# ReLU row sums: an opening block without its barrier, and another split of the last rows between ScalarE and VectorE

## The chip, the cores and the metric

The kernel runs on one core of a Trainium2 chip. The metric is the device time of one execution in microseconds (us). All executions quoted here are of the fast state, at a granted clock of 1.0. The kernel before had a median of 161.21 us (161.05 to 161.3, 3 runs). A profile is of one execution; its span runs from the first instruction to the last and is, in the kernel before, 1.3 to 1.4 us shorter than the execution's time.

## The reference

```python
x = np.random.randn(32, 512, 1024).astype(np.float32)
def reference(x):
    relu_x = np.maximum(x, 0)
    return np.sum(relu_x, axis=-1).astype(np.float32)
```

It reads 67.11 MB and writes 0.07 MB: 16384 rows of 1024 columns, one sum for each row. The data lie in 128 partitions (the lanes on which an engine works in parallel), so every partition has 128 rows.

## The kernel before

All loads are issued by SyncE, into three buffers of 16 rows per partition and, at the end, into two small tiles for pieces of a row. A load raises a semaphore, a counter for which the engines wait, once it has landed. In the body ScalarE clamps 7 to 16 rows at a time and VectorE reduces them. For the last rows each engine does whole rows by itself, with the sum as an accumulator output of the same instruction; the profile shows a second record for it, the accumulator read, which writes the sum out. The last four rows of a partition are treated apart: one for ScalarE, one for VectorE, the "split row", and the last row, which is ScalarE's. Of the split row 360 columns come with the two whole rows, the other 260 and 404 after the last row, as two loads of their own.

```python
TAIL = [8, 4]
PIECES = [360, 260, 404]
EARLY = 1
# ... (cut) ...
    first = PIECES[0]
    loaded = load(
        buf[:, :, :].rearrange("p c d -> p (c d)")[:, c * D : (c + 2) * D + first],
        rows(m, 3).rearrange("p c d -> p (c d)")[:, : 2 * D + first],
    )
    act_row(buf[:, c, :], m, loaded)
    dve_row(buf[:, c + 1, :], res[:, m + 1 : m + 2], loaded)
    last_loaded = load(buf[:, c + 3, :], rows(m + 3, 1)[:, 0, :])
    arrived = []
    col = first
    for part, w in zip(parts, PIECES[1:]):
        arrived.append(load(part[:, :w], rows(m + 2, 1)[:, 0, col : col + w]))
        col += w
    sums_done = n_act, n_dve
    act_row(buf[:, c + 3, :], m + 3, last_loaded)
    # ... the stores of the other rows' sums ...
    last, w = parts[-1], PIECES[-1]
    dve_row(buf[:, c + 2, :first], last[:, w : w + 1], None)
    for i in range(1, extra):
        dve_row(parts[i - 1][:, :], last[:, w + i : w + i + 1], arrived[i - 1])
    nc.vector.wait_ge(sems.dve, n_dve)
    nc.vector.tensor_scalar(out=last[:, :], in0=last[:, :], scalar1=0.0, scalar2=None,
        op0=MAX, op1=ADD, accum_out=res[:, NT - 2 : NT - 1],
    ).wait_op(arrived[-1], 16, "sem-ge").then_inc(sems.dve, 1)
    store(NT - 2, 2, n_act, n_dve)
```

The sums of the earlier pieces are written into extra columns behind the last piece (they are never negative, so the clamp leaves them alone), and the last instruction adds all up. It must wait for VectorE's own earlier writes, hence the `wait_ge` on VectorE's own semaphore.

The opening block of the program holds a barrier: each engine drains and waits for all the others. `EARLY = 1` puts the first load ahead of it:

```python
def issue_ahead_of_the_barrier(tc, n_loads):
    # ... (cut) ...
    loads = [i for i in body if i.engine == SP][:n_loads]
    for i in loads:
        body.remove(i)
    at = next(n for n, i in enumerate(opening) if i.engine == SP)
    opening[at:at] = loads
```

Of the kernel before, what the change touches and what calls it, by code (L numbers as in the profile page):

```python
# [4 lines left out]
F32 = mybir.dt.float32  # L5
# [12 lines left out]


TAIL = [8, 4]  # L20
PIECES = [360, 260, 404]

EARLY = 1

# [1 line left out]
def kernel(tc: tile.TileContext, x: bass.AP, out: bass.AP):  # L26
    nc = tc.nc
    sems = Semaphores(tc)

    tc.close()  # L30
    tc.compile()
    nc.cur_bb = nc.bb_map[tc.start_bb_name]
    body = nc.cur_bb.bb.instructions
    ends = list(body)
    body.clear()
    n_stores = relu_sum(nc, sems, x, out)
    body.extend(ends)


    nc.cur_bb = nc.bb_map[tc.start_bb_name + "_end"]  # L40
    nc.cur_bb.bb.instructions.clear()
    nums = sorted(s.num for s in (*sems.loads, sems.act, sems.dve))
    cleared = range(nums[0], nums[-1] + 1)
    assert len(cleared) == len(nums)
    nc.sync.sem_clear(cleared)
    nc.sync.wait_ge(sems.stored, 16 * n_stores).then_inc(sems.stored, -16 * n_stores)
    issue_ahead_of_the_barrier(tc, EARLY)


class Semaphores:  # L50
    def __init__(self, tc: tile.TileContext):
        n = len(TWO) + len(TAIL) + 1 + len(PIECES)
        self.loads = [tc.alloc_semaphore(f"load{i}") for i in range(n)]
        self.act = tc.alloc_semaphore("act")
        self.dve = tc.alloc_semaphore("dve")
        self.stored = tc.alloc_semaphore("stored")


def relu_sum(nc, sems: Semaphores, x: bass.AP, out: bass.AP):
    x_flat = x.flatten_outer_dims()  # L60
    N, D = x_flat.shape
    NT = N // P
    NB = len(TWO)
    assert N == P * NT == P * ROWS * (NB + 1)
    assert sum(TAIL) == ROWS - 4 and sum(PIECES) == D

    bufs = [nc.alloc_sbuf_tensor(f"io{i}", [P, ROWS, D], F32) for i in range(NBUF)]
    res = nc.alloc_sbuf_tensor("res", [P, NT], F32)
    extra = len(PIECES) - 1
    parts = [  # L70
        nc.alloc_sbuf_tensor(f"piece{i + 1}", [P, w + extra * (i + 1 == extra)], F32)
        for i, w in enumerate(PIECES[1:])
    ]


    N1 = P * ROWS
    xf = x_flat[:N1].rearrange("(p m) d -> p m d", p=P)
    xv = x_flat[N1:].rearrange("(p m) d -> p m d", p=P)
    o_flat = out.rearrange("b s -> (b s)")
    of = o_flat[:N1].rearrange("(p m) -> p m", p=P)  # L80
    ov = o_flat[N1:].rearrange("(p m) -> p m", p=P)

    def rows(m, n):
        if m < ROWS:
            return xf[:, m : m + n, :]
        return xv[:, m - ROWS : m - ROWS + n, :]

    def sums(m, n):
        if m < ROWS:
            return of[:, m : m + n], res[:, m : m + n]  # L90
        return ov[:, m - ROWS : m - ROWS + n], res[:, m : m + n]

    n_load = n_act = n_dve = n_store = 0

    def load(dst, src, after=None):
        nonlocal n_load
        dma = nc.sync.dma_start(out=dst, in_=src)  # L97
        if after:
            dma.wait_op(sems.dve, after[1], "sem-ge")
        dma.then_inc(sems.loads[n_load], 16)  # L100
        n_load += 1
        return sems.loads[n_load - 1]

    def store(m, n, act, dve):
        nonlocal n_store
        dst, src = sums(m, n)
        nc.sync.wait_ge(sems.act, act)
        nc.sync.dma_start(out=dst, in_=src).wait_op(sems.dve, dve, "sem-ge").then_inc(
            sems.stored, 16
        )  # L110
        n_store += 1

    def clamp(ap, loaded):
        nonlocal n_act
        i = nc.scalar.activation(out=ap, in_=ap, func=RELU)  # L115
        if loaded is not None:
            i.wait_op(loaded, 16, "sem-ge")
        i.then_inc(sems.act, 1)
        n_act += 1

    def total(ap, m, n):
        nonlocal n_dve
        nc.vector.tensor_reduce(  # L123
            out=res[:, m : m + n], in_=ap, axis=mybir.AxisListType.X, op=ADD
        ).wait_op(sems.act, n_act, "sem-ge").then_inc(sems.dve, 1)
        n_dve += 1

    def act_row(ap, m, loaded):
        nonlocal n_act
        i = nc.scalar.activation(  # L130
            out=ap, in_=ap, func=RELU, accum_out=res[:, m : m + 1]
        )
        if loaded is not None:
            i.wait_op(loaded, 16, "sem-ge")
        i.then_inc(sems.act, 1)
        n_act += 1

    def dve_row(ap, accum_out, loaded):
        nonlocal n_dve
        i = nc.vector.tensor_scalar(  # L140
            out=ap,
            in0=ap,
            scalar1=0.0,
            scalar2=None,
            op0=MAX,
            op1=ADD,
            accum_out=accum_out,
        )
        if loaded is not None:
            i.wait_op(loaded, 16, "sem-ge")  # L150
        i.then_inc(sems.dve, 1)
        n_dve += 1

    freed = []
    m = 0
    for j in range(NB):
        buf = bufs[j % NBUF]
        loaded = load(buf[:, :, :], rows(m, ROWS), j >= NBUF and freed[j - NBUF])
        c = 0
        act_waits = dve_waits = loaded  # L160
        for n in TWO[j]:
            clamp(buf[:, c : c + n, :], act_waits)
            total(buf[:, c : c + n, :], m + c, n)
            act_waits = None
            c += n
        for _ in range(ACT[j]):
            act_row(buf[:, c, :], m + c, act_waits)
            act_waits = None
            c += 1
        for _ in range(DVE[j]):  # L170
            dve_row(buf[:, c, :], res[:, m + c : m + c + 1], dve_waits)
            dve_waits = None
            c += 1
        assert c == ROWS
        freed.append((n_act, n_dve))
        m += ROWS


    buf = bufs[NB % NBUF]
    c = 0  # L180
    for n in TAIL:
        loaded = load(
            buf[:, c : c + n, :], rows(m, n), None if c else freed[NB - NBUF]
        )
        for i in range(n):
            if i % 2 == 0 or (n == 8 and i == 7):
                act_row(buf[:, c, :], m, loaded if i == 0 else None)
            else:
                dve_row(buf[:, c, :], res[:, m : m + 1], loaded if i == 1 else None)
            c += 1  # L190
            m += 1

    first = PIECES[0]
    loaded = load(
        buf[:, :, :].rearrange("p c d -> p (c d)")[:, c * D : (c + 2) * D + first],
        rows(m, 3).rearrange("p c d -> p (c d)")[:, : 2 * D + first],
    )
    act_row(buf[:, c, :], m, loaded)
    dve_row(buf[:, c + 1, :], res[:, m + 1 : m + 2], loaded)
    last_loaded = load(buf[:, c + 3, :], rows(m + 3, 1)[:, 0, :])  # L200
    arrived = []
    col = first
    for part, w in zip(parts, PIECES[1:]):
        arrived.append(load(part[:, :w], rows(m + 2, 1)[:, 0, col : col + w]))
        col += w
    sums_done = n_act, n_dve
    act_row(buf[:, c + 3, :], m + 3, last_loaded)



    store(0, ROWS, *freed[0])
    store(ROWS, NT - ROWS - 2, *sums_done)

    last, w = parts[-1], PIECES[-1]
    dve_row(buf[:, c + 2, :first], last[:, w : w + 1], None)
    for i in range(1, extra):
        dve_row(parts[i - 1][:, :], last[:, w + i : w + i + 1], arrived[i - 1])
    nc.vector.wait_ge(sems.dve, n_dve)  # L218
    nc.vector.tensor_scalar(  # L219
        out=last[:, :],  # L220
        in0=last[:, :],
        scalar1=0.0,
        scalar2=None,
        op0=MAX,
        op1=ADD,
        accum_out=res[:, NT - 2 : NT - 1],
    ).wait_op(arrived[-1], 16, "sem-ge").then_inc(sems.dve, 1)
    n_dve += 1
    store(NT - 2, 2, n_act, n_dve)
    return n_store  # L230


def issue_ahead_of_the_barrier(tc: tile.TileContext, n_loads: int):


    SP = mybir.EngineType.SP
    blocks = tc.nc.main_func.blocks
    opening = blocks[0].instructions
    body = next(b for b in blocks if b.name == tc.start_bb_name).instructions
    loads = [i for i in body if i.engine == SP][:n_loads]  # L240
    for i in loads:
        assert isinstance(i, mybir.InstDMACopy)
# [3 lines that stand above are left out]
# [30 lines left out]
```

## Time and profile before

| | before |
|---|---|
| span of the profiled execution | 159.6 us |
| DMA queue's packet time, share of the span | 98.1% |
| VectorE busy / ScalarE busy | 117.5 / 104.2 us |
| first compute (ScalarE starts on the first load) | 21.73 us |
| both engines start on the load with the two whole rows | 155.36 us |
| last sum ends | 158.17 us |

Below, "the row's start" is ScalarE's start on the first of the last four rows (155.36 here), and "the tail" is the time from there to the end of the last sum on either engine: 158.17 - 155.36 = 2.81 us. The profile lines are shown in the prediction.

### The profile page before, as it was taken

How to read it: one execution, taken by the hardware profiler on the slowest of the kernel's cores; microseconds unless marked ns; L12 is line 12 of the kernel's file. 1: busy time of each engine (PE TensorE's matmuls, PEld its weight loads, DVE VectorE, ACT ScalarE, POOL GpSimd, SP SyncE). 2: the span in 40 equal slices, each digit the busy share in tenths (PEclk: the TensorE clock that was granted, in tenths of full speed). 3: DMA queues.
4: the chain of work that ended last, by engine and by line, in shares of the span. 5: the costliest groups of instructions: out<-in, count | busy, mean ns of one | idle time of the engine just before them, and what ended most of it. 6: DMA issues, size and time to landing. Idle time of an engine off the chain costs nothing.

```text
span 159.6 us, 129 instructions
## 1 busy us (share of the span) xinstructions
DVE 117.5 (74%) x41; ACT 104.2 (65%) x50; POOL 0.2 (0%) x4
## 2 busy tenths in 40 slices
DVE  0000000009999499994999999999999999999986
ACT  3000059990799708996099941999339992499985
POOL 0000000000000000000000000000000000000000
DMA  7996996996996998979969969969969969798994
GB/s 263 525 525 263 525 526 263 525 525 263 526 493 296 525 411 378 525 328 460 526 279 509 525 263 526 525 263 525 525 263 525 509 279 525 337 452 386 412 405 127
DMA packets 2304, 67.18 MB, mean 421 GB/s; under 512 B 640, under 2 KB 896, under 8 KB 1024
## 3 DMA queue, kind: packets, MB, share of 16 engines
q1 hardware_dynamic: 2304, 67.18, 98.1%
HBM read 67.11 MB, written 0.07 MB: 421 GB/s over the span
## 4 chain that ended last, share of the span: by engine, by line
DMA 43%; DVE 34%; ACT 17%; another core or an unknown queue 3%; SPq 0%; issue 0%; DVEq 0%
DMA io<-in_x_dram 43%; DVE res L123 32%; ACT io L115 17%; DVE io L140 1%; SPq L97 0%; DVE piece L219 0%; DVE piece L140 0%; DVEq L218 0%
## 5 line engine op out<-in xcount | busy, mean ns | idle before, releaser
L123 DVE TENSOR_REDUCE res<-io 128x8 f32<-128x8192 f32 (+2 forms) x9 | 101.1, 11286 | 39.9 <-ACT io L115 39.9
L115 ACT ACTIVATE io<-io 128x8192 f32<-128x8192 f32 (+2 forms) x9 | 81.7, 9111 | 46.9 <-DMA io<-in_x_dram 46.9
L130 ACT ACTIVATE io<-io 128x1024 f32<-128x1024 f32 x20 | 20.9, 1045 | 5.9 <-DMA io<-in_x_dram 5.7
L140 DVE TENSOR_SCALAR_CACHE_REDUCE io<-io 128x1024 f32<-128x1024 f32 (+1 forms) x14 | 15.5, 1165 | 0.7 <-DMA io<-in_x_dram 0.6
L130 ACT ACTIVATION_READ_ACCUMULATOR io<-io 128x1 f32 x20 | 3.8, 188 | 0.0
L115 ACT ACT_TABLE_LOAD x1 | 1.3, 1283 | 0.8 <-PEq L260 0.8
L140 DVE DVE_READ_ACCUMULATOR io<-io 128x1 f32 x14 | 1.2, 82 | 0.0
L219 DVE TENSOR_SCALAR_CACHE_REDUCE piece<-piece 128x406 f32<-128x406 f32 x1 | 0.6, 576 | 0.1
L140 DVE TENSOR_SCALAR_CACHE_REDUCE piece<-piece 128x260 f32<-128x260 f32 x1 | 0.4, 424 | 0.0
L260 POOL MEMSET const-bfloat16-1.0<- 128x1 bf16 x1 | 0.1, 102 | 0.0
L260 POOL MEMSET const-uint8-127<- 128x1 uint8 x1 | 0.1, 102 | 0.0
L260 POOL MEMSET const-float32-0.0<- 128x1 f32 x1 | 0.1, 99 | 0.2 <-issue 0.2
L260 POOL MEMSET const-float32-1.0<- 128x1 f32 x1 | 0.1, 99 | 0.0
L140 DVE DVE_READ_ACCUMULATOR piece<-piece 128x1 f32 x1 | 0.1, 83 | 0.0
L219 DVE DVE_READ_ACCUMULATOR piece<-piece 128x1 f32 x1 | 0.1, 82 | 0.0
## 6 DMA issues: line engine op xcount, KB each, us to landing
io<-in_x_dram SPq DMA_DIRECT2D x1, 4096.0 KB, 21.6
io<-in_x_dram SPq DMA_DIRECT2D x1, 2048.0 KB, 26.1
io<-in_x_dram SPq DMA_DIRECT2D x1, 1204.0 KB, 28.6
io<-in_x_dram SPq DMA_DIRECT2D x1, 512.0 KB, 29.4
piece<-in_x_dram SPq DMA_DIRECT2D x1, 202.0 KB, 29.3
piece<-in_x_dram SPq DMA_DIRECT2D x1, 130.0 KB, 29.3
io<-in_x_dram SPq DMA_DIRECT2D x7, 26.9
out_dram<-res SPq DMA_DIRECT2D x1, 55.0 KB, 1.6
```

Source lines behind the costliest of these rows:

```text
L115: i = nc.scalar.activation(out=ap, in_=ap, func=RELU)
L123: nc.vector.tensor_reduce(out=res[:, m : m + n], in_=ap, axis=mybir.AxisListType.X, op=ADD).wait_op(sems.act, n_act, "sem-ge").then_inc(se ...
L130: i = nc.scalar.activation(out=ap, in_=ap, func=RELU, accum_out=res[:, m : m + 1])
L140: i = nc.vector.tensor_scalar(out=ap, in0=ap, scalar1=0.0, scalar2=None, op0=MAX, op1=ADD, accum_out=accum_out,)
L219: nc.vector.tensor_scalar(out=last[:, :], in0=last[:, :], scalar1=0.0, scalar2=None, op0=MAX, op1=ADD, accum_out=res[:, NT - 2 : NT - 1],) ...
L260: nc = _bacc.Bacc("TRN2", target_bir_lowering=False, num_devices=1)
```

## The change

Its intent is twofold: no barrier at the start, so that nothing waits for it; and a shorter way from the last landing to the last sum. ScalarE takes 180 columns of the split row, the row's last 190 columns come in one load with the last row (they are adjacent in memory; the load has 607 KB), and the middle comes last as pieces of 220 and 224 columns, so that the last instruction has 228 columns instead of 406.

```diff
-PIECES = [360, 260, 404]
+ACT_PIECE, DVE_PIECE, END_PIECE = 180, 210, 190
+PIECES = [220, 224]
 ...
+    loaded = load(flat[:, at : at + b], src[:, :b])
+    act_row(buf[:, c, :], res[:, m : m + 1], loaded)
+    sums_act = n_act
+    act_row(flat[:, at + split : at + a], others[0], None)
+    piece_act = n_act
+    dve_row(buf[:, c + 1, :], res[:, m + 1 : m + 2], loaded)
+    sums_dve = n_dve
+    dve_row(flat[:, at + a : at + b], others[1], None)
+    loaded = load(flat[:, at + end : at + 4 * D], src[:, end:])
+    act_row(buf[:, c + 3, :], res[:, m + 3 : m + 4], loaded)
+    nc.vector.wait_ge(sems.act, piece_act)
+    dve_row(flat[:, at + end : at + 3 * D], others[2], loaded)
+    arrived = []
+    for part, n in zip(parts, PIECES):
+        arrived.append(load(part[:, :n], src[:, b : b + n]))
+        b += n
 ...   (two stores, cut)
+    for i in range(len(PIECES) - 1):
+        dve_row(parts[i][:, :], others[3 + i], arrived[i])
 ...   (the last instruction and the last store stay as they were; most removed lines are cut)
+    for i in list(opening):
+        if isinstance(i, (mybir.InstDrain, mybir.InstEventSemaphore)):
+            opening.remove(i)
```

More of the change, by code (lines that the diff above doesn't have):

```diff
@@ L46 @@
     nc.sync.wait_ge(sems.stored, 16 * n_stores).then_inc(sems.stored, -16 * n_stores)
-    issue_ahead_of_the_barrier(tc, EARLY)
+    open_without_barrier(tc, EARLY)
 class Semaphores:
     def __init__(self, tc: tile.TileContext):
-        n = len(TWO) + len(TAIL) + 1 + len(PIECES)
+        n = len(TWO) + len(TAIL) + 2 + len(PIECES)
         self.loads = [tc.alloc_semaphore(f"load{i}") for i in range(n)]
@@ L64, in relu_sum @@
     assert N == P * NT == P * ROWS * (NB + 1)
-    assert sum(TAIL) == ROWS - 4 and sum(PIECES) == D
+    assert sum(TAIL) == ROWS - 4 and ACT_PIECE + DVE_PIECE + END_PIECE + sum(PIECES) == D
     bufs = [nc.alloc_sbuf_tensor(f"io{i}", [P, ROWS, D], F32) for i in range(NBUF)]
     res = nc.alloc_sbuf_tensor("res", [P, NT], F32)
-    extra = len(PIECES) - 1
+    extra = len(PIECES) + 2
     parts = [
-        nc.alloc_sbuf_tensor(f"piece{i + 1}", [P, w + extra * (i + 1 == extra)], F32)
-        for i, w in enumerate(PIECES[1:])
+        nc.alloc_sbuf_tensor(f"piece{i}", [P, w + extra * (i + 1 == len(PIECES))], F32)
+        for i, w in enumerate(PIECES)
     ]
@@ L126, in total, with act_row @@
         n_dve += 1
-    def act_row(ap, m, loaded):
+    def act_row(ap, accum_out, loaded):
         nonlocal n_act
-        i = nc.scalar.activation(
-            out=ap, in_=ap, func=RELU, accum_out=res[:, m : m + 1]
-        )
+        i = nc.scalar.activation(out=ap, in_=ap, func=RELU, accum_out=accum_out)
         if loaded is not None:
@@ L166, in relu_sum @@
         for _ in range(ACT[j]):
-            act_row(buf[:, c, :], m + c, act_waits)
+            act_row(buf[:, c, :], res[:, m + c : m + c + 1], act_waits)
             act_waits = None
@@ L186, in relu_sum @@
             if i % 2 == 0 or (n == 8 and i == 7):
-                act_row(buf[:, c, :], m, loaded if i == 0 else None)
+                act_row(buf[:, c, :], res[:, m : m + 1], loaded if i == 0 else None)
             else:
@@ L191, in relu_sum @@
             m += 1
-    first = PIECES[0]
-    loaded = load(
-        buf[:, :, :].rearrange("p c d -> p (c d)")[:, c * D : (c + 2) * D + first],
-        rows(m, 3).rearrange("p c d -> p (c d)")[:, : 2 * D + first],
-    )
-    act_row(buf[:, c, :], m, loaded)
-    dve_row(buf[:, c + 1, :], res[:, m + 1 : m + 2], loaded)
-    last_loaded = load(buf[:, c + 3, :], rows(m + 3, 1)[:, 0, :])
-    arrived = []
-    col = first
-    for part, w in zip(parts, PIECES[1:]):
-        arrived.append(load(part[:, :w], rows(m + 2, 1)[:, 0, col : col + w]))
-        col += w
-    sums_done = n_act, n_dve
-    act_row(buf[:, c + 3, :], m + 3, last_loaded)
-    store(0, ROWS, *freed[0])
-    store(ROWS, NT - ROWS - 2, *sums_done)
-    last, w = parts[-1], PIECES[-1]
-    dve_row(buf[:, c + 2, :first], last[:, w : w + 1], None)
-    for i in range(1, extra):
-        dve_row(parts[i - 1][:, :], last[:, w + i : w + i + 1], arrived[i - 1])
+    flat = buf[:, :, :].rearrange("p c d -> p (c d)")
+    src = rows(m, 4).rearrange("p c d -> p (c d)")
+    at = c * D
+    split = 2 * D
+    a, b = split + ACT_PIECE, split + ACT_PIECE + DVE_PIECE
+    end = split + D - END_PIECE
+    last, w = parts[-1], PIECES[-1]
+    others = [last[:, w + i : w + i + 1] for i in range(extra)]
+    loaded = load(flat[:, at : at + b], src[:, :b])
[3 more added lines that the diff above has]
+    piece_act = n_act
+    dve_row(buf[:, c + 1, :], res[:, m + 1 : m + 2], loaded)
+    sums_dve = n_dve
[4 more added lines that the diff above has]
+    dve_row(flat[:, at + end : at + 3 * D], others[2], loaded)
+    arrived = []
+    for part, n in zip(parts, PIECES):
+        arrived.append(load(part[:, :n], src[:, b : b + n]))
+        b += n
+    assert b == end
+    store(0, ROWS, *freed[0])
+    store(ROWS, NT - ROWS - 2, sums_act, sums_dve)
+    for i in range(len(PIECES) - 1):
+        dve_row(parts[i][:, :], others[3 + i], arrived[i])
     nc.vector.wait_ge(sems.dve, n_dve)
@@ L230, in relu_sum, with open_without_barrier @@
     return n_store
-def issue_ahead_of_the_barrier(tc: tile.TileContext, n_loads: int):
+def open_without_barrier(tc: tile.TileContext, n_loads: int):
     SP = mybir.EngineType.SP
```

## The prediction

> **What bounds the kernel now.** I read the page first, then the chain of work that ended last in order of time, then the timeline of the last 8 us and of the first two, and last the DMA issues.
>
> The page's load figures come first:
>
> ```profile
> DMA  7996996996996998979969969969969969798994
> ...
> q1 hardware_dynamic: 2304, 67.18, 98.1%
> HBM read 67.11 MB, written 0.07 MB: 421 GB/s over the span
> ```
>
> The DMA engines are busy 98.1% of the 159.6 us span. VectorE (74%) and ScalarE (65%) are not the bound of the body. Everything that the body computes lies beside the loads.
>
> The chain, in order of time (start us, us, what), shows where the bound starts and where it stops:
>
> ```profile
> 0.72 0.07 issue
> 0.79 40.24 DMA io<-in_x_dram
> 41.04 0.02 issue
> ...
> 126.77 28.57 DMA io<-in_x_dram
> 155.34 0.02 issue
> 155.36 1.68 DVE io L140 x4
> 157.03 0.43 DVE piece L140 x2
> 157.47 0.03 issue
> 157.49 0.02 DVEq L218
> 157.51 0.07 issue
> 157.58 0.58 DVE piece L219 x2
> ```
>
> Two things are to be seen. At the start, the load on the chain is the second one, issued at 0.79 after the barrier; it lands at 41.03, while the first one, issued at 0.00, has landed by 21.73, where ScalarE starts on it. The loads therefore stand in a queue: an 8.39 MB load lands every 41.04 - 21.73 = 19.3 us. At the end, from 155.34 on, a stretch of 159.6 - 155.3 = 4.3 us follows the large loads: a whole row on VectorE, three pieces of the split row, and the closing store. Only this stretch can be changed by another split.
>
> The timeline of that stretch (start us, us, engine line op tile) is what my sums rest on:
>
> ```profile
> 155.36 1.06 ACT L130 ACTIVATE io<-io 128x1024 f32<-128x1024 f32 x1 [0.45 <-DMA io<-in_x_dram]
> 155.36 1.22 DVE L140 TENSOR_SCALAR_CACHE_REDUCE io<-io 128x1024 f32<-128x1024 f32 x1 [0.57 <-DMA io<-in_x_dram]
> ...
> 156.50 0.52 DVE L140 TENSOR_SCALAR_CACHE_REDUCE io<-io 128x360 f32<-128x360 f32 x1
> ...
> 156.65 1.06 ACT L130 ACTIVATE io<-io 128x1024 f32<-128x1024 f32 x1
> ...
> 157.02 0.42 DVE L140 TENSOR_SCALAR_CACHE_REDUCE piece<-piece 128x260 f32<-128x260 f32 x1
> 157.37 0.08 DVE L140 DVE_READ_ACCUMULATOR piece<-piece 128x1 f32 x1
> 157.58 0.58 DVE L219 TENSOR_SCALAR_CACHE_REDUCE piece<-piece 128x406 f32<-128x406 f32 x1
> 157.62 0.19 ACT L130 ACTIVATION_READ_ACCUMULATOR io<-io 128x1 f32 x1
> 158.09 0.08 DVE L219 DVE_READ_ACCUMULATOR piece<-piece 128x1 f32 x1
> ```
>
> VectorE ends at 158.17, ScalarE at 157.81, so ScalarE has 0.36 us to spare. The store goes at 158.19 and takes 1.4 us to land.
>
> The landings come from the DMA issues (KB each, us from issue to landing):
>
> ```profile
> io<-in_x_dram SPq DMA_DIRECT2D x1, 512.0 KB, 29.4
> piece<-in_x_dram SPq DMA_DIRECT2D x1, 202.0 KB, 29.3
> piece<-in_x_dram SPq DMA_DIRECT2D x1, 130.0 KB, 29.3
> ```
>
> The timeline of the SyncE queue has the two pieces issued at 127.73 and 128.22, so the 260 columns land at 157.0 and the 404 columns at 157.5; two rows and 360 columns (1204 KB) land at 155.34 by the chain, and the last row (512 KB) just before ScalarE starts on it, at about 156.63. All are issued some 29 us ahead, so issue costs nothing; they land as fast as the queue moves.
>
> **What the Trainium skill says.** "VectorE: DVE Perf Modes", in the section on the trn2 errata, says that each instruction that reads SBUF pays a fixed latency, so that many small tiles pay it many times. The trace agrees: 1214 ns for 1024 columns and 424 ns for 260 give 790/764 = 1.034 ns per column and a fixed 155 ns; the next instruction starts about 70 ns before such a one ends, at the start of its accumulator read. "ScalarE: Activation LUTs", section "What ACT_TABLE_LOAD costs", gives 186 ns + 0.833 ns per column with immediate operands, with an overlap of about 93 ns. The trace agrees: 1042 ns for 1024 columns, where that makes 1039. "DMA: Bandwidth & Descriptors", section "Where 436 GB/s comes from", puts the ceiling of the DMA ports at 435 GB/s; 8.39 MB in 19.33 us here are 434 GB/s, so nothing in the body can go faster. I use no page for the opening barrier.
>
> **The change part by part.**
>
> *The barrier.* In the program before, each engine drains and waits on it in the opening block; only the first load stands ahead of it. Without it the second load can be issued at about 0.38 instead of 0.74 (the first issue takes 0.38), and ScalarE's table load (1.28 us from 0.79) can start earlier. Neither is on the path: the second load queues behind the first, which keeps the DMA engines until about 20 us, and ScalarE has nothing to do until 21.73. I set it to 0.00 us. The constants that GpSimd writes, which the barrier had guarded, are written by 0.43 us; the race check passes.
>
> *The stream's end.* The order becomes: two rows and 390 columns (1219 KB), then the row's last 190 columns with the last row (607 KB), then 220 columns (110 KB) and 224 (112 KB). The number of loads stays the same. The landings before give about 1.30 us for 512 KB and 0.37 for 130 KB, which is 0.93/382 = 2.43 ns per KB and some 0.05 us per load (202 KB would then make 0.54, measured 0.5). So the first lands 15 KB later, at 155.38; the second 1.53 after it, at 156.91; the 220 columns 0.32 later, at 157.23; the 224 columns 0.32 later, at 157.55. The last landing is thus where it was, within 0.05.
>
> *ScalarE.* It starts its row at 155.40, the new 180 columns at 155.40 + 1.04 - 0.09 + 0.10 = 156.45 (the spacing of its rows is 1.04), where they take 186 + 150 = 0.34 us and an accumulator read, ending at about 156.87. Its last row, which started at 156.65 before, now waits for the 607 KB, so it starts at 156.93 and ends 1.16 later (156.65 to 157.81 before): 158.09. That uses 0.28 of its 0.36 us to spare.
>
> *VectorE.* It starts its row at 155.40, the 210 columns at 156.54 and is free of them by about 156.9. The 190 columns wait for the same 607 KB and start at 156.93; they take 155 + 196 = 0.35, so the next may start 0.28 later, at 157.21; the 220 columns land at 157.23 and start at 157.25. From there to the last piece: before, 157.02 to 157.58 = 0.56 for 260 columns, part of which is the wait for the write of the sums; with 40 columns less 0.52. So the last piece starts at 157.77, after its landing at 157.55. It has 228 columns instead of 406, which is 178 x 1.034 = 0.18 us less: 0.59 with its accumulator read becomes 0.41. End: 158.18.
>
> *Sum.* Before: 158.17. After: 158.18, plus the same store. The 0.18 us that the last piece gives up is lost before it: the chain of small pieces now starts when the 607 KB land, 0.27 us later than the last row did, and each small piece pays its fixed time. VectorE sums 2050 columns after 155.34 before and 1872 after (0.18 us less), but in five instructions instead of four (0.155 - 0.07 more), and it waits for data in between.
>
> **The rivals.** (a) *The gain intended*: if the last landing sets the end and the chain of small pieces keeps ahead of it, the last piece starts 0.07 after 157.55 and ends at 158.03, a gain of 0.14 us, so 161.07. For it: the last piece now starts only 0.08 after its landing. Against it: the 0.52 us from 220-column start to last start, which is longer than the 0.32 between their landings. (b) *ScalarE becomes the bound*: its end, 158.09 by my sum, lies 0.09 below VectorE's. If the 607 KB land 0.15 later than I think, both end later together, as both wait for that load: +0.15 us, so 161.35. For it: one packet of 4856 bytes at the end of each row instead of 4096. Against it: the bytes are the same in sum. (c) *The barrier's time was on the path*: if the DMA engines started earlier without it, at most the 0.36 us between 0.38 and 0.74 could be gained, so 160.85. Against it: the first load stands ahead of the barrier already and the second is queued 19 us. (d) *VectorE's new wait for ScalarE's 180 columns*: done at 156.87, before the 607 KB at 156.91, so free; it would cost only as far as ScalarE is later than that.
>
> **Range and chances.** My sum says no change; (a) and (c) pull down a little and (b) up a little, so I take 161.15 us. The three runs of before lie within 161.05 to 161.30, and runs of one kernel agree to some tenths; with the rivals' -0.35 to +0.15 the range of 8 in 10 is 160.85 to 161.4. Two per cent are 3.2 us; no term here is a tenth of it. Faster 0.01, same 0.98, slower 0.01.
>
> **What would show it right or wrong.** In the profile after: the second load issued about 0.4 us after the first, with first compute still at 21.7; the two large loads of the end landing at about 155.4 and 156.9, which show as the starts of two rows on ScalarE; the 190 columns starting with that last row; the last piece of 228 columns taking 0.39 us and starting at about 157.77, held by VectorE's own queue and not by a load; ScalarE's last accumulator read ending 0.1 us before VectorE's. The prediction is wrong if the first compute comes earlier than 21.5 (c), if the last piece starts within 0.08 us of its landing and the end is 0.1 us or more earlier (a), or if ScalarE's end sets the store (b).

## The result, and the profile after

The changed kernel has a median of 161.19 us (161.12 to 161.51, 6 runs), the kernel before 161.19 us (161.05 to 161.3, its 6 runs). Ratios here are the mean time of one kernel's fast runs over that of the other's of the same rounds, so not quite the ratio of the medians quoted: 1.0004, 95% interval 0.9991 to 1.0017.

The page after, its DMA queue (packets, MB, share of 16 engines' span) and traffic:

```profile
q1 hardware_dynamic: 2304, 67.18, 97.8%
HBM read 67.11 MB, written 0.07 MB: 420 GB/s over the span
```

The loads still fill the span. The span of this one execution is 159.9 us, 0.3 more than before's, although the medians are equal. Where that 0.3 is, the timeline of the first compute shows (start us, us, engine line op tile), before and then after:

```profile
21.73 13.86 ACT L115 ACTIVATE io<-io 128x16384 f32<-128x16384 f32 x1 [19.66 <-DMA io<-in_x_dram]
```

```profile
22.03 13.86 ACT L117 ACTIVATE io<-io 128x16384 f32<-128x16384 f32 x1 [20.63 <-DMA io<-in_x_dram]
```

The first load landed 0.30 us later, and everything after it is later by as much. Whether that is the change's doing is a question for the experiments. The chain that ended last, after, in order of time:

```profile
0.43 40.89 DMA io<-in_x_dram
...
127.05 28.58 DMA io<-in_x_dram
...
155.66 1.52 DVE io L140 x4
157.18 0.02 DVEq L211
157.20 0.07 issue
157.27 0.36 DVE io L140 x2
157.63 0.31 DVE piece L140 x2
...
157.97 0.02 DVEq L226
...
158.05 0.40 DVE piece L227 x2
```

The second load is issued at 0.43 instead of 0.79, and its landing (0.43 + 40.89 = 41.32) is no earlier for it. In the tail a new link stands between VectorE's pieces: L211 is the new `wait_ge`, with which VectorE's queue waits for ScalarE's 180 columns until 157.20; an issue of 0.07 us follows it. The timeline of the tail, after:

```profile
155.66 1.06 ACT L132 ACTIVATE io<-io 128x1024 f32<-128x1024 f32 x1 [0.46 <-DMA io<-in_x_dram]
...
156.71 0.34 ACT L132 ACTIVATE io<-io 128x180 f32<-128x180 f32 x1
...
156.95 0.19 ACT L132 ACTIVATION_READ_ACCUMULATOR io<-io 128x1 f32 x1
157.09 0.08 DVE L140 DVE_READ_ACCUMULATOR io<-io 128x1 f32 x1
157.19 1.06 ACT L132 ACTIVATE io<-io 128x1024 f32<-128x1024 f32 x1
157.27 0.35 DVE L140 TENSOR_SCALAR_CACHE_REDUCE io<-io 128x190 f32<-128x190 f32 x1
...
157.54 0.38 DVE L140 TENSOR_SCALAR_CACHE_REDUCE piece<-piece 128x220 f32<-128x220 f32 x1
157.84 0.08 DVE L140 DVE_READ_ACCUMULATOR piece<-piece 128x1 f32 x1
158.05 0.39 DVE L227 TENSOR_SCALAR_CACHE_REDUCE piece<-piece 128x228 f32<-128x228 f32 x1
158.15 0.19 ACT L132 ACTIVATION_READ_ACCUMULATOR io<-io 128x1 f32 x1
158.37 0.08 DVE L227 DVE_READ_ACCUMULATOR piece<-piece 128x1 f32 x1
```

The last piece does take 0.39 us instead of 0.58. But it starts 158.05 - 155.66 = 2.39 us after the row's start, where it was 157.58 - 155.36 = 2.22 before. In the kernel before, VectorE went on to its 260 columns at 157.02, after this accumulator read of the 360 columns:

```profile
156.95 0.08 DVE L140 DVE_READ_ACCUMULATOR io<-io 128x1 f32 x1
```

In the kernel after, the way from the read at 157.09 to the 190 columns at 157.27 is longer. The tail is 158.45 - 155.66 = 2.79 us, against 2.81. ScalarE ends at 158.34. The landings (KB each, us from issue to landing):

```profile
io<-in_x_dram SPq DMA_DIRECT2D x1, 607.0 KB, 29.6
...
piece<-in_x_dram SPq DMA_DIRECT2D x1, 112.0 KB, 29.2
piece<-in_x_dram SPq DMA_DIRECT2D x1, 110.0 KB, 29.4
```

The two pieces are issued from 128.01 on, the second half a microsecond later, so they land at about 157.4 and 157.7: both before VectorE gets to them (157.54 and 158.05).

### The profile page after: what moved, and what is told of

The parts are those of the page before. It is cut to its first block, busy times and chain, and to the rows that moved or that the text cites. A ratio compares the mean times of both kernels' runs of the same rounds, so it can differ in the third digit from the quotient of the medians.

```text
span 159.9 us, 123 instructions
## 1 busy us (share of the span) xinstructions
DVE 117.4 (73%) x43; ACT 104.6 (65%) x52; POOL 0.2 (0%) x4
## 2 busy tenths in 40 slices
DMA packets 2304, 67.18 MB, mean 420 GB/s; under 512 B 640, under 2 KB 896, under 8 KB 1024
## 4 chain that ended last, share of the span: by engine, by line
DMA 43%; DVE 34%; ACT 17%; another core or an unknown queue 3%; SPq 1%; issue 0%; DVEq 0%
DMA io<-in_x_dram 43%; DVE res L125 32%; ACT io L117 17%; DVE io L140 1%; SPq L99 1%; DVE piece L227 0%; DVE piece L140 0%; DVEq L226 0%; DVEq L211 0%
## 5 line engine op out<-in xcount | busy, mean ns | idle before, releaser
L132 ACT ACTIVATE io<-io 128x1024 f32<-128x1024 f32 (+1 forms) x21 | 21.2, 1010 | 5.8 <-DMA io<-in_x_dram 5.7
L140 DVE TENSOR_SCALAR_CACHE_REDUCE io<-io 128x1024 f32<-128x1024 f32 (+2 forms) x15 | 15.7, 1100 | 0.8 <-DMA io<-in_x_dram 0.6
```

The costliest lines, as they stand in the source:

```text
L132: i = nc.scalar.activation(out=ap, in_=ap, func=RELU, accum_out=accum_out)
L140: i = nc.vector.tensor_scalar(out=ap, in0=ap, scalar1=0.0, scalar2=None, op0=MAX, op1=ADD, accum_out=accum_out,)
```

## The experiments

Twelve programs ran, two of them repeats, in four groups; each group shares its runs of the kernel before on one chip. For each profile I took three numbers from the timeline: the first compute, the row's start, and the end of the last sum.

| profile | barrier | first compute | row's start | last sum ends | tail | first compute to last sum |
|---|---|---|---|---|---|---|
| before | yes | 21.73 | 155.36 | 158.17 | 2.81 | 136.44 |
| after | no | 22.03 | 155.66 | 158.45 | 2.79 | 136.42 |
| e1_tail_only | yes | 21.90 | 155.55 | 158.34 | 2.79 | 136.44 |
| e2_open_only | no | 21.97 | 155.59 | 158.39 | 2.80 | 136.42 |
| e3_after_again | no | 21.99 | 155.61 | 158.40 | 2.79 | 136.41 |
| e4_before_again | yes | 21.86 | 156.04 | 158.84 | 2.80 | 136.98 |
| e5_late_barrier | yes | 22.78 | 156.39 | 159.19 | 2.80 | 136.41 |
| e6_late_open | no | 21.84 | 155.46 | 158.26 | 2.80 | 136.42 |
| e7_no_gather | no | 21.93 | 155.60 | 158.27 | 2.67 | 136.34 |
| e8_row_first | yes | 21.98 | 155.61 | 158.42 | 2.81 | 136.44 |
| e9_dve_180 | no | 22.18 | 155.81 | 158.63 | 2.82 | 136.45 |
| e10_widths | no | 21.86 | 155.57 | 158.38 | 2.81 | 136.52 |
| e11_wait_last | no | 22.01 | 155.65 | 158.39 | 2.74 | 136.38 |
| e12_widths_wait_last | no | 21.89 | 155.61 | 158.32 | 2.71 | 136.43 |

The last column is free of the chance in the start. In seven of the eight profiles that have the old or the new split unaltered (before, after, e1 to e3, e5, e6) it lies between 136.41 and 136.44; the eighth, e4, is half a microsecond off. So it mostly scatters by 0.03 us, and the tail of one split by 0.01; each line of the table is one execution.

**e1_tail_only**: the new split, the barrier kept.

```diff
-    for i in list(opening):
-        if isinstance(i, (mybir.InstDrain, mybir.InstEventSemaphore)):
-            opening.remove(i)
```

> The new split of the last rows with the barrier kept. Theory A (both parts are worth nothing; the 0.3 us by which the profile after starts later is chance of the execution): ratio to before 0.999 to 1.001; from ScalarE's start on its row of the 1219 KB load to the end of VectorE's last accumulator read 2.8 us, as in the profile after (155.66 to 158.45) and before (155.36 to 158.17). Theory B (the new tail gains 0.1 to 0.2 us and the opening without the barrier costs as much, by a later start of the loads): ratio 0.9985 to 0.9993, first compute at 21.7 us as before.

Measured: 161.39 us (161.23 to 161.43) against 161.22, ratio 1.001 (0.9997 to 1.0022). Tail 2.79, first compute 21.90. Theory B is out: the tail gains 0.02 us, not 0.1 to 0.2. The time is a little high, but not within the program's instructions: its profiled execution took 161.40 us with a span of 159.8, which leaves 1.6 us outside the span instead of 1.3 to 1.4. The one other program with the new split and the barrier, e8, shows the same 1.6. It holds for every execution: 1.46 to 1.63 us outside the span in e1 and 1.58 to 1.62 in e8, against 1.30 to 1.42 in all others. What makes it so in these two programs is open. So with the new split, taking the barrier away did go with a shorter time: all five executions of e1 (161.23 to 161.43) are above all five of e3 (161.05 to 161.22), the same kernel without the barrier in the same rounds. The difference lies outside the span, where the profiles don't show what takes it.

**e2_open_only**: the old split, the barrier removed (the three lines above added to the kernel before).

> The barrier removed, the old split of the last rows. Theory A: ratio 0.999 to 1.001; first compute anywhere from 21.6 to 22.1 us. Theory B: first compute at about 22.0 us as in the profile after, and 0.2 to 0.3 us more than before (ratio 1.001 to 1.002). Rival (c) of the prediction (barrier time was on the path): ratio 0.998 or less.

Measured: 161.23 us (161.1 to 161.42) against 161.22, ratio 1.0003 (0.9991 to 1.0016). Rival (c), a gain of 0.36 us from the barrier, is out for the old split. The first compute at 21.97 falls near what theory B expected, so it alone doesn't rule out a later start; but the time shows no cost of 0.2 to 0.3 us.

**e3_after_again**: the changed kernel once more, no edit.

> The changed kernel once more, for its scatter. Theory A: ratio within 0.999 to 1.001, first compute may fall at 21.7 this time. Theory B: first compute at 22.0 again.

Measured: 161.16 us (161.05 to 161.22), ratio 0.9996 (0.9983 to 1.001), first compute 21.99, which is close to theory B's 22.0. The times side with theory A.

**e4_before_again**: the kernel before once more, no edit.

> The kernel before once more, for the scatter of its profile. Theory A: its first compute lies between 21.6 and 22.1 us, not always at 21.73, and the span moves with it; tail of 2.81 us. Theory B: first compute at 21.7 again and span 159.6.

Measured: 161.22 us (161.04 to 161.68), ratio to its own other runs 1.0009 (0.9996 to 1.0021). The profiled execution was the slow end of these: 161.68 us, span 160.3. Its first compute is at 21.86, its tail 2.80, and the missing half microsecond lies in between: 156.04 - 21.86 = 134.18 us from first compute to the row's start, against 155.36 - 21.73 = 133.63 in the first profile of the same kernel. The loads alone can scatter by that much.

Of the fourteen profiles, five have the barrier. Their first computes, counted from the issue of the first load, are 21.73, 21.86, 21.90, 21.98 and 22.05 (e5: 22.78 - 0.73); the nine without it lie between 21.84 and 22.18. The ranges overlap, with means of 21.90 and 21.97. A difference of about 0.1 us in the start is not excluded, but the 0.30 of the first pair is mostly chance.

**e5_late_barrier** and **e6_late_open**: the kernel before with its first load not ahead of the barrier; and the same without a barrier (the three lines of the change added).

```diff
-EARLY = 1
+EARLY = 0
```

> The kernel before, but with its first load behind the barrier too (EARLY = 0). Theory A (the barrier is worth nothing only because the first load stands ahead of it): everything moves later by the barrier, 0.5 to 0.7 us; about 161.85 us, ratio 1.003 to 1.0045. Rival (the engines wait for the runtime anyway, and the barrier costs nothing wherever the load stands): ratio 0.999 to 1.001.

> The same without the barrier: old split, EARLY = 0, the load in the body. Theory A: the load is issued at once after a branch; within 0.15 us of before (ratio 0.9993 to 1.001), so 0.4 to 0.7 us below the run with the barrier. Rival: as the run with the barrier. First compute against the issue of the first load: 21.9 to 22.1 if taking the barrier away makes the slowest DMA engine start later (the three executions without it had 21.97, 21.99 and 22.03, the three with it 21.73, 21.86 and 21.90), 21.6 to 22.1 if that is chance.

Measured: e5 161.94 us (161.77 to 162.12) against 161.15, ratio 1.0049 (1.0034 to 1.0064); e6 161.19 us, ratio 1.0003 (0.9987 to 1.002). The timeline of e5 shows the cost:

```profile
0.73 1.32 SPq L97 DMA_DIRECT2D io<-in_x_dram  x3
```

Its first load is issued at 0.73 us instead of 0.00, and 161.94 - 161.15 = 0.79 us are lost, a little more than the 0.7 that I had expected at most. So the barrier does cost three quarters of a microsecond where a load waits for it. In the kernel before, no load that mattered did: the gain had been taken already by the edit that put one load ahead. Without a barrier that edit is superfluous (e6).

**e7_no_gather**: wrong (relative error 0.07): the last piece doesn't add the other sums and so needs no wait for them.

```diff
-    nc.vector.wait_ge(sems.dve, n_dve)
     nc.vector.tensor_scalar(
-        out=last[:, :],
-        in0=last[:, :],
+        out=last[:, :w],
+        in0=last[:, :w],
```

> The changed kernel, wrong on purpose: the last piece does not add up the other sums, so it need not wait for their writes. Theory A (after the 607 KB VectorE's own chain sets the end): the last piece starts with the accumulator read of the piece before it, 2.18 us after ScalarE's start on its row of the 1219 KB load instead of 2.39; VectorE ends at 2.58 instead of 2.79, ScalarE at 2.68 then sets the store, and the time from that row's start to the end of the last sum falls by 0.11 us. Rival (the last landing or ScalarE already sets the end): it stays at 2.79.

Measured: tail 2.67 us as theory A has it; time 161.05 us (160.93 to 161.19), ratio 0.9994 (0.9979 to 1.0009). Its timeline:

```profile
157.79 0.08 DVE L140 DVE_READ_ACCUMULATOR piece<-piece 128x1 f32 x1
157.79 0.38 DVE L226 TENSOR_SCALAR_CACHE_REDUCE piece<-piece 128x224 f32<-128x224 f32 x1
158.08 0.19 ACT L132 ACTIVATION_READ_ACCUMULATOR io<-io 128x1 f32 x1
```

The last piece starts with the accumulator read before it, 157.79 - 155.60 = 2.19 us after the row's start; VectorE ends at 158.17, ScalarE at 158.27. So in the changed kernel VectorE's chain sets the end, and waiting for its own writes is 0.21 us of it (157.84 to 158.05 in the profile after). The kernel before has the same 0.21 (157.37 to 157.58), so this wait is not what the change costs. Taking it away gains only 0.12 because ScalarE is next. From first compute to last sum the gain is 0.08 (136.34 against 136.42).

**e9_dve_180**: ScalarE's 180 columns given back to VectorE, and the wait for them gone.

```diff
-ACT_PIECE, DVE_PIECE, END_PIECE = 180, 210, 190
+ACT_PIECE, DVE_PIECE, END_PIECE = 0, 390, 190
 ...
-    act_row(flat[:, at + split : at + a], others[0], None)
-    piece_act = n_act
 ...   (the sums' places are renumbered)
-    nc.vector.wait_ge(sems.act, piece_act)
```

> The changed kernel with ScalarE's 180 columns given back to VectorE, in one piece of 390 columns, and so without the wait for ScalarE. Theory A (these columns only fill time in which VectorE would wait for the 607 KB): VectorE is through with the 390 at 1.63 us after its row's start, against the 607 KB's landing at 1.51, and starts the 190 columns there instead of at 1.61; from row start to the last sum 2.80 to 2.83 us instead of 2.79. Rival (the 0.19 us that ScalarE takes over were gained on the path): 2.96 to 2.99.

Measured: tail 2.82; 161.24 us (161.16 to 161.44), ratio 1.0007 (0.9992 to 1.0022). Its timeline:

```profile
157.44 0.35 DVE L140 TENSOR_SCALAR_CACHE_REDUCE io<-io 128x190 f32<-128x190 f32 x1
```

The 190 columns start 157.44 - 155.81 = 1.63 us after the row's start with all 390 columns on VectorE, and 157.27 - 155.66 = 1.61 with ScalarE's help. The 180 columns moved to ScalarE, with the wait that they bring, are worth 0.02 us at this start and 0.03 at the end, not their 0.19. (Without that wait, in e11 below, the 190 columns start at 1.51.)

**e8_row_first**: the last row loaded ahead of the 190 columns, each by its own load; barrier kept.

```diff
-    loaded = load(flat[:, at + end : at + 4 * D], src[:, end:])
+    loaded = load(flat[:, at + 3 * D : at + 4 * D], src[:, 3 * D :])
     act_row(buf[:, c + 3, :], res[:, m + 3 : m + 4], loaded)
+    loaded = load(flat[:, at + end : at + 3 * D], src[:, end : 3 * D])
 ...   (one semaphore more; the barrier's three lines removed as in e1)
```

> The new split with the barrier kept, and with the last row loaded ahead of the 190 columns, each by a load of its own. Theory A (VectorE's chain from the 190 columns on sets the end, ScalarE has 0.1 us to spare): ScalarE's last row starts 1.40 us after the start of its row before instead of 1.50 to 1.53 and ends at 2.56 instead of 2.68, but the 190 columns land no earlier, so VectorE ends at 2.79 to 2.84 as before. Rival (b of the prediction, ScalarE's last row sets the end): it falls to 2.67.

Measured: ScalarE's last row starts 1.39 us after the row's start and ends at 2.53; VectorE ends at 2.81; 161.48 us (161.3 to 161.52), ratio 1.0013 (0.9997 to 1.003), with the 1.6 us outside the span already seen in e1. Freeing ScalarE by 0.15 us changes nothing, so rival (b) is out as the cause here.

**e10_widths**: other widths.

```diff
-ACT_PIECE, DVE_PIECE, END_PIECE = 180, 210, 190
-PIECES = [220, 224]
+ACT_PIECE, DVE_PIECE, END_PIECE = 240, 180, 120
+PIECES = [180, 304]
```

> The changed kernel with other widths: ScalarE 240 and VectorE 180 columns of the first load, 120 with the last row, then 180 and 304. Theory A: the load with the last row lands 0.05 us earlier against the one before, the two pieces ahead of the last are 110 columns shorter (0.11 us), the last 80 longer (0.08): from ScalarE's row start to the end of the last sum about 2.74 us instead of 2.79, and the last piece then starts close to its own landing; no width gains more. Time 161.1 to 161.25, ratio 0.999 to 1.0005. Rival (the last piece's width sets the end, as the change meant): 80 columns more cost 0.08 us, 2.87.

Measured: tail 2.81, not 2.74, and not the rival's 2.87 either; 161.21 us, ratio 1.0003 (0.9988 to 1.0018). Its timeline tells why I missed:

```profile
156.92 0.19 ACT L132 ACTIVATION_READ_ACCUMULATOR io<-io 128x1 f32 x1
...
157.23 0.28 DVE L140 TENSOR_SCALAR_CACHE_REDUCE io<-io 128x120 f32<-128x120 f32 x1 [0.17 <-ACT io L132]
```

VectorE stood idle for 0.17 us until ScalarE had done its 240 columns: it starts 157.23 - 157.11 = 0.12 us after the end of ScalarE's accumulator read, as it does in the profile after (157.27 - 157.14 = 0.13). The wait that I had held to be free was on the path, and the next two runs test that.

**e11_wait_last** and **e12_widths_wait_last**: the wait for ScalarE's piece moved to the instruction that reads its sum, in the changed kernel and in e10.

```diff
-    nc.vector.wait_ge(sems.act, piece_act)
     dve_row(flat[:, at + end : at + 3 * D], others[2], loaded)
 ...
+    nc.vector.wait_ge(sems.act, piece_act)
     nc.vector.wait_ge(sems.dve, n_dve)
```

> The changed kernel with VectorE's wait for ScalarE's 180 columns moved from ahead of the 190 columns to ahead of the last piece, which is the one that reads that sum. Theory A with the wait counted (in the profile after, the 190 columns started 0.11 us after their landing, where a row starts 0.03 after its own): the 190 columns start 1.53 us after ScalarE's row start instead of 1.61, and all after them comes 0.08 earlier; the last sum ends at 2.71 instead of 2.79, ScalarE at 2.68 all but sets the end. Rival (the wait is free, the landing holds the 190 columns): 2.79.

> The widths 240, 180, 120, 180 and 304 with the same move of the wait. In the run of these widths the 120 columns started 0.21 us after their landing, held by ScalarE. Theory A with the wait counted: they start at 1.48 instead of 1.66 us; the last piece then starts at its own landing, 2.18, instead of 2.33, and the last sum ends at 2.66 instead of 2.81; the time is 0.1 us below the kernel before, ratio 0.9985 to 1.0003, which the runs' scatter may hide. Rival (the widths themselves cost it): 2.81 stays.

Measured: e11 161.19 us (161.07 to 161.23) against 161.27, ratio 0.9992 (0.998 to 1.0005), tail 2.74; e12 161.18 us, ratio 0.9999 (0.9985 to 1.0012), tail 2.71. The timeline of e11:

```profile
157.16 1.06 ACT L132 ACTIVATE io<-io 128x1024 f32<-128x1024 f32 x1
157.16 0.35 DVE L140 TENSOR_SCALAR_CACHE_REDUCE io<-io 128x190 f32<-128x190 f32 x1
```

Both engines now start on the 607 KB load together, 157.16 - 155.65 = 1.51 us after the row's start; VectorE's was 1.61. Of the 0.10 us, 0.05 reach the end (2.79 to 2.74, where 2.71 was expected; 136.42 to 136.38 from the first compute). Ahead of the last piece two waits now stand instead of one (0.05 us in the queue by the chain of e11, 0.02 in that of the profile after), and it starts 0.24 us after the accumulator read before it instead of 0.21; the rest of the difference is spacing of hundredths that I did not take apart. In e12 the tail is shorter still (2.66 was expected), but its larger first load lands later, 155.61 - 21.89 = 133.72 us after the first compute instead of 133.63, so in sum it gains nothing (136.43). e11 is the best correct version in the last column, by 0.04 and 0.06 us against the first profiles of the two kernels, which is little more than the column's scatter. Its interval contains 1, so I do not call it faster.

## Why the prediction was right

The prediction was 161.15 us in a range of 160.85 to 161.4, with "same" at 0.98; the median is 161.19. By its steps:

- *The barrier at 0.00 us*: right for what happens inside the program. Removing it alone gave 1.0003 (e2). The reason held too: the second load was issued 0.36 us earlier (0.43 instead of 0.79; the 0.38 and 0.74 of the prediction are each 0.05 early) and landed no earlier, and e5 shows that the barrier costs 0.79 us as soon as the first load stands behind it. Not foreseen and not explained: the 0.2 us outside the span of the programs with the new split and the barrier (e1, e8).
- *The stream's end*: the 607 KB were to come 1.53 us after the first of the tail's loads, and ScalarE's two starts show just that (157.19 - 155.66). The small pieces came faster than my fit: by the trace's semaphore increments the last landed 157.71 - 155.63 = 2.08 us after the first, where I had 2.17. As VectorE was not waiting for them, that changed nothing.
- *ScalarE*: predicted end 2.69 us after the row's start (158.09 - 155.40), measured 2.68. The prediction's estimate for 180 columns, 186 + 150 = 336 ns by the formula of "ScalarE: Activation LUTs" (section "What ACT_TABLE_LOAD costs"), fits the trace's 0.34 us.
- *VectorE*: predicted end 2.78 us after the row's start, measured 2.79, in part by luck: the 190 columns started 0.08 late (1.61 instead of 1.53), and 0.05 of that was won back because the 220 columns then did not wait for their landing, as I had thought they would (0.27 us after the 190, not 0.32). The rest went in hundredths: from the 220 columns to the last piece I had 0.52 us and it took 0.51, and from there to the end 0.40 instead of 0.41.
- *Rival (d), the step that failed*: "done at 156.87, before the 607 KB at 156.91, so free; it would cost only as far as ScalarE is later than that". ScalarE was not later: its accumulator read ended at 157.14, and the 607 KB landed at 157.17. Yet VectorE started only at 157.27, while ScalarE started on the same load at 157.19. What I left out is that the way through the wait is longer: from the end of ScalarE's read to VectorE's start it takes 0.12 to 0.13 us, in each of the six profiles that have this wait (after, e1, e3, e7, e8, e10), and from a landing to a start 0.02 to 0.03. ScalarE would have had to be done about 0.10 us before the landing. e11 took the wait out of that place and the start moved by 0.10 us.
- *Rival (a), the intended gain*: out. The last piece started 158.05 - 157.71 = 0.34 us after its landing; not the landing but VectorE's chain held it, as e7 shows. Ahead of the last piece both kernels sum 620 columns of the split row on VectorE (360 + 260 before, 210 + 190 + 220 after), but the last piece starts 2.39 us after the row's start instead of 2.22. About 0.10 of the difference is idle time ahead of the 190 columns (157.27 - 157.09 = 0.18 after the start of the accumulator read before them, where the 260 columns before had 157.02 - 156.95 = 0.07). About 0.08 is the instruction more, by my estimate from the prediction's 1.034 ns per column: 157.54 - 157.27 = 0.27 us from the 190 columns to the next start, of which the columns take 0.20. Together that is nearly all of the 0.19 us that the last piece gave up.
- *"No term here is a tenth of it"* (of 2% of the time, 3.2 us): a slip in the sum, as rival (c) was set at up to 0.36 us. It changes nothing in the forecast.
- *First compute "still at 21.7"*: it was 22.03. I had taken one execution's start for the kernel's. The experiments show 21.73 to 22.05 with the barrier and 21.84 to 22.18 without it.

## What to carry to other kernels

Before removing a wait, look at what would go ahead of it: here the barrier was worth 0.79 us with the first load behind it and nothing that the profiles show with that load in front. Cutting the last instruction short gains only what the chain of small pieces before it doesn't give back; draw that chain with its waits. A wait for another engine that was done 0.03 us before the data delayed the next start by 0.10 us here, and an engine's wait on its own fresh result was 0.21 us, more than the columns saved. Moving the first of them to the instruction that reads the result shortened the tail by 0.05 us (e11). And where one profile of each kernel differs by a few tenths, measure from an event behind the chance part (here from the first compute), and take more than one profile: seven of eight then agreed within 0.03 us, and the eighth was off by 0.5.

## What the Trainium skill lacked or had wrong

- "DMA: Bandwidth & Descriptors" has the 16 engines finish independently (section "Why a DMA increments its semaphore by 16 and not by 1") but not how far apart they finish on loads that SyncE issues. The trace records each load's 16 increments: in the profile after, fifteen had come by 21.73 us and the last at 22.01; before, all by 21.71. The gap stayed: on the load that ends near 138 us the last two increments came at 137.85 and 138.07 (the record doesn't name the engine). First computes lay between 21.73 and 22.18 us, and in thirteen of fourteen profiles this was nearly all of the scatter.
- "VectorE: DVE Perf Modes", section "The DRAIN you can't avoid", finds that a semaphore after each of eight copies costs nothing extra. That doesn't carry over to a wait for sums that the engine has just written: here the last piece starts 0.21 us after the start of the accumulator read before it, and together with it when the wait is taken out (e7).
- No page that I read has the time from one engine's accumulator read to another engine's start through a wait: 0.12 to 0.13 us from ScalarE's to VectorE's in six profiles, against 0.02 to 0.03 from a landing to a start.
- "ScalarE: Activation LUTs" names the accumulator output but gives it no price: its read is 187 ns on ScalarE in these traces (82 ns on VectorE). Back to back, rows of 1024 columns with it follow each other by 1.04 us, the length of the ACTIVATE alone, so the read overlaps the ACTIVATEs around it.
- No page that I read has the cost of a kernel's own opening barrier: the first load was issued at 0.73 us behind it and at 0.00 without it.
- No page explains the 1.6 us, instead of 1.3 to 1.4, outside the instruction span of e1 and e8; the runs leave it open.
